# W_down on two bank sets, emptied into four output blocks, and tail tiles with roots of their own

## The chip, the cores and the metric

One core of a Trainium2 chip runs the kernel. The metric is the device time of one execution in microseconds (us). One execution was also recorded by the hardware profiler; the times in the rows below count from the start of its span.

## What is computed

One decoder layer on x of 1024 positions by 1024 channels, in fp32: two token mixers side by side, their projection W_out, and an MLP, each with a norm before and after it. The change touches the last line of it alone:

```
h = rms_norm(x, norm_ffn_pre[i])
f = jnp.square(jax.nn.relu(jnp.einsum("bld,df->blf", h, w_up[i])))
x = x + rms_norm(jnp.einsum("blf,fd->bld", f, w_down[i]), norm_ffn_post[i])
```

W_down is 4096 x 1024, f is 1024 x 4096. rms_norm divides each row by the root of its mean square and multiplies by a weight.

## The kernel before, in words

Every dense product is done with split operands: each fp32 operand is a high part (rounded) and a low part (the rest), and mm3 (L123) issues three matmuls, high x high, high x low, low x high.

The W_down product (L1097 to L1316) goes over 4096 inner columns in eight groups of 512. Seven of them use Winograd's form of Strassen's scheme: the product of 2 x 2 blocks with seven block products instead of eight. The outputs are four blocks of 512 x 512 (two row halves, two column halves). With P1 to P7 the block products, the four blocks are P1 + P2, P1 + P6 + P5 + P3, P1 + P6 + P7 - P4 and P1 + P6 + P7 + P5. The combinations of f were spilled to memory (fsp) by the stage before; those of W_down (t1 to t4) are formed here, as differences of blocks on VectorE (w_block, L1128). The groups are gathered in sets SG (L1101): one group, then two, two, two; the eighth group is multiplied plainly in the tail.

In the loop at L1210 each step is one block product of one group: 4 row tiles x 2 inner blocks x 3 matmuls = 24 matmuls of 512 columns. Two steps ahead of it, d_prep (L1163) makes the operands ready: f_load (L1144) brings a piece of f into one of two staging buffers (L1217 issues it three steps ahead), ScalarE rounds it to the high part, GpSimd forms the low part (f_piece, L1148, three pairs of buffers fh and fl); ScalarE and VectorE do the same for the block of W_down. A product has a bank set of 128 x 2048 in PSUM, two sets in turn (tag pd, L1222). ORD (L1103) is the order of the products, and MORE (L1104) names those that continue on the bank set of another: P2 is added to P1 in the bank, P3 to P5. After the last group of a set, flush (L1184) empties the bank set into one of seven accumulators accs (L1097), by a copy on ScalarE in the first set and by an addition on VectorE later; in the last set, five additions among the accumulators, the final sums, form the four blocks.

The tail (L1296 on) takes 8 row tiles of 128 x 1024, each in two halves. For each half: 12 matmuls of the eighth group (pl, L1304, eight banks, in the place of the two bank sets), VectorE adds them to the block, ScalarE sums the squares, GpSimd multiplies by the norm's weight. When a tile has both halves, VectorE computes the reciprocal root by an integer seed and three Newton steps (chain, L1247, rstd_steps, L136), and finishes each half: multiply by the root, add x, and an output transfer (finish, L1260). TAIL (L1245) takes the first six tiles in pairs: operations of the chain then have two columns a partition and two tensor inputs; the last two have chains of their own, whose Newton steps use the form with one tensor input. The chain and the finishes of a tile are queued (todo) and issued between later halves, up to a number of steps given to some (L1268); VectorE's order in the tail is the order of the code (L1296). In the stage ahead, the scheduler sets the order on each engine.

Of the kernel before, what the change touches and what calls it, by code (L numbers as in the profile page):

```python
# [8 lines left out]
F32 = mybir.dt.float32  # L9
# [6 lines left out]
P = 128  # L16
SEQ = 1024
D = 1024
# [15 lines left out]
N_STAGE = 2  # L34
# [6 lines left out]
N_CARRY = 2  # L41
# [15 lines left out]
def hymba_kernel(ctx, tc, x, norm_mix_pre, w_in, gm_ln_w, gm_ln_b, gm_w_s, gm_b_s,  # L57
# [24 lines left out]
    pe, act, dve, pool = [Engine(e) for e in (nc.tensor, nc.scalar, nc.vector, nc.gpsimd)]  # L82

    def pool_of(stack, name, **k):
        return stack.enter_context(tc.tile_pool(name=name, bufs=1, reuse_waits="tile", **k))
# [7 lines left out]
    stage = pool_of(uctx, "stage")  # L93
# [36 lines left out]
    def rstd_base(ss, n):  # L130
        nsmall[0] += 1
        b = const.tile([P, 1], F32, tag="rb", bufs=4, name=f"rb{nsmall[0]}")
        dve.tensor_scalar(b, ss, 0.5 / n, 0.5 * EPS, op0=ALU.mult, op1=ALU.add)
        return b

    def rstd_steps(ss, n, base=None):  # L136
        nsmall[0] += 1
        i = nsmall[0]
        w = ss.shape[-1]
        v = const.tile([P, w], F32, tag=f"rv{w}", bufs=2 if w == 1 else 1, name=f"rv{i}")  # L140
        r = const.tile([P, w], F32, tag=f"rr{w}", bufs=4 if w == 1 else 1, name=f"rr{i}")
        t = const.tile([P, w], F32, tag=f"rt{w}", bufs=2 if w == 1 else 1, name=f"rt{i}")
        ti = const.tile([P, w], I32, tag=f"rti{w}", bufs=2 if w == 1 else 1, name=f"rti{i}")
        yield r
        if base is None:
            dve.tensor_scalar(v, ss, 0.5 / n, 0.5 * EPS, op0=ALU.mult, op1=ALU.add)
        else:
            dve.tensor_scalar(v, ss, 0.5 / n, base, op0=ALU.mult, op1=ALU.add)
        yield
        dve.tensor_scalar(ti, v.bitcast(I32), 1, None, op0=ALU.logical_shift_right)  # L150
        yield
        dve.tensor_scalar(r.bitcast(I32), ti, -1.0, RSQRT_SEED, op0=ALU.mult, op1=ALU.add)
        for _ in range(3):
            yield
            if w == 1:
                dve.tensor_scalar(t, r, r, v, op0=ALU.mult, op1=ALU.mult)
            else:
                dve.tensor_mul(t, v, r)
                dve.tensor_mul(t, t, r)
            yield  # L160
            if w == 1:
                dve.tensor_scalar(r, t, 1.5, r, op0=ALU.subtract, op1=ALU.mult)
            else:
                dve.scalar_tensor_tensor(r, t, 1.5, r, op0=ALU.subtract, op1=ALU.mult)
# [87 lines left out]
    for what in PRO_LOADS:  # L252
# [4 lines left out]
        else:  # L257
            t = int(what)
# [611 lines left out]
    def tt(eng, out_, a, b, op):  # L870
        eng.tensor_tensor(out_, a, b, op=op)

    def sub(eng, out_, a, b):
        tt(eng, out_, a, b, ALU.subtract)

    def add(eng, out_, a, b):
        tt(eng, out_, a, b, ALU.add)
# [213 lines left out]
    dpool = pool_of(ctx, "dpool")  # L1091
    apool = pool_of(ctx, "apool")
# [1 line left out]
    now["nwp"] = pool_of(ctx, "nw2")  # L1094
    pctx2 = stack()
    psum2 = pool_of(pctx2, "psum2", space=bass.MemoryType.PSUM)
    accs = {i: apool.tile([P, 4, 512], F32, name=f"acc{i}") for i in range(1, 8)}  # L1097
    last = N_GROUP - 1


    SG = [(0,), (1, 2), (3, 4), (5, 6), (last,)]  # L1101
    sg_of = {g: (n, gs.index(g)) for n, gs in enumerate(SG) for g in gs}
    ORD = (1, 5, 2, 3, 6, 7, 4)  # L1103
    MORE = {2: 1, 3: 5}  # L1104
    raws, wts, pcs = {}, {}, {}
    wr_loads = []

# [20 lines left out]
    def w_block(g, key):  # L1128
        if key[0] == "b":
            return rows(g, int(key[1]) - 1)[:, :, int(key[2]) - 1, :]  # L1130
        if (g, key) not in wts:
            one, two = {"t1": ("b12", "b11"), "t2": ("b22", "t1"), "t3": ("b22", "b12"),
                        "t4": ("t2", "b21")}[key]
            a_, b_ = w_block(g, one), w_block(g, two)
            t_ = a_ if key == "t4" else dpool.tile([P, 2, 512], F32, tag="wt", bufs=4, name=f"w{key}_{g}")
            sub(dve, t_, a_, b_)
            wts[g, key] = t_
        return wts[g, key]
# [3 lines left out]
    frs = {}  # L1142

    def f_load(name, src):  # L1144
        frs[name] = stage.tile([P, 2, 512], F32, tag="ws", bufs=N_STAGE, name="fr" + name)
        nc.sync.dma_start(frs[name], src)

    def f_piece(name, tags=("fh", "fl"), bufs=3):  # L1148
        fr = frs[name]
        hl = piece([P, 2, 512], "f" + name) if tags is None else \  # L1150
            tuple(dpool.tile([P, 2, 512], F32R, tag=t_, bufs=bufs, name=f"f{i}" + name)
                  for i, t_ in enumerate(tags))
        split(*hl, fr)
        return hl
# [13 lines left out]

    seq = [(n, g, i) for n, gs in enumerate(SG[:-1]) for i in ORD for g in gs]
    us, ffs = [], []  # L1170
# [10 lines left out]
    floads = [lambda g=g, i=i: d_load(g, i) for n, g, i in seq]  # L1181
    floads += [lambda i=i: last_load(i) for i in range(4)]

    def flush(n, i, ps):  # L1184
        a_ = accs
        if n == 0:
            act.copy(a_[i], ps)
            return
        if n == len(SG) - 2 and i == 4:
            sub(dve, a_[4], a_[4], ps)  # L1190
            return
        add(dve, a_[i], ps, a_[i])
        if n < len(SG) - 2:
            return
        if i == 6:
            add(dve, a_[6], a_[6], a_[1])
            add(dve, a_[3], a_[3], a_[6])
        elif i == 7:
            add(dve, a_[7], a_[7], a_[6])
            sub(dve, a_[4], a_[7], a_[4])  # L1200
            add(dve, a_[5], a_[5], a_[7])

    w_load(0, 0)
    floads[0]()
# [5 lines left out]
    for m, (n, g, i) in enumerate(seq):  # L1210
        gs = SG[n]
        k = m - seq.index((n, gs[0], ORD[0]))
        if k == len(gs):
            w_load(n + 1, 0)
        elif k == 5 * len(gs) + 1:
            w_load(n + 1, 1)
        floads[m + 3]()  # L1217
        preps[m + 2]()
        (fh, fl), (h, l) = pcs[g, i]
        if g == gs[0]:  # L1220
            banks[i] = banks[MORE[i]] if i in MORE else \
                psum2.tile([P, 4, 512], F32, tag="pd", bufs=2, name=f"pd{n}_{i}")  # L1222
        ps = banks[i]
        for t in range(4):
            tsl = slice(t * P, (t + 1) * P)
            for q in range(2):
                mm3(ps[:, t, :], fh[:, q, tsl], fl[:, q, tsl], h[:, q, :], l[:, q, :],
                    g == gs[0] and q == 0 and i not in MORE, g == gs[-1] and q == 1,
                    skip_group_check=i in MORE)
        if g == gs[-1]:  # L1230
            flush(n, i, ps)
    for m in range(len(seq) + 2, len(preps)):
        if m + 1 < len(preps):
            floads[m + 1]()
# [4 lines left out]
    psum3 = pool_of(ctx, "psum3", space=bass.MemoryType.PSUM)  # L1239

    def acc(t, dh):
        return accs[((2, 3), (4, 5))[t // 4][dh]][:, t % 4, :]

    xqs, sss, chains, rs = [], {}, {}, {}
    TAIL = ((0, 1), (2, 3), (4, 5), (6,), (7,))  # L1245

    def chain(ts):  # L1247

        nsmall[0] += 1
        w = len(ts)  # L1250
        v = const.tile([P, w], F32, tag=f"tv{w}", bufs=2, name=f"tv{nsmall[0]}")
        dve.tensor_tensor(v, sss[ts][:, :, 0], sss[ts][:, :, 1], op=ALU.add)
        yield
        steps = rstd_steps(v, D)
        r = next(steps)
        for j, t in enumerate(ts):
            rs[t] = r[:, j:j + 1]
        yield from steps
# [9 lines left out]
    def some(k):  # L1268
        while k and todo:
            if todo[0]() == "done":  # L1270
                todo.pop(0)
            k -= 1
# [23 lines left out]
    dve.held = True  # L1296
    for ts in TAIL:
        ss = sss[ts] = const.tile([P, len(ts), 2], F32, tag=f"st{len(ts)}", bufs=4, name=f"ssy{ts[0]}")
        for j, t in enumerate(ts):
            tsl = slice(t * P, (t + 1) * P)  # L1300
            for dh in range(2):
                ds_ = slice(dh * 512, (dh + 1) * 512)
                a_ = acc(t, dh)
                ps = psum3.tile([P, 512], F32, tag="pl", bufs=8, name=f"pl{t}{dh}")  # L1304
                for i in range(4):
                    mm3(ps, ffs[i][0][:, tsl], ffs[i][1][:, tsl], us[i][0][:, dh, :],
                        us[i][1][:, dh, :], i == 0, i == 3)
                add(dve, a_, ps, a_)
                junk = now["tok"].tile([P, 512], BF16, tag="junk", bufs=1, name=f"yj{t}{dh}")
                act.activation(junk, a_, AF.Square, accum_out=ss[:, j, dh:dh + 1])  # L1310
                pool.tensor_tensor(a_, a_, wfpost[:, ds_], op=ALU.mult)
                some(6 if len(ts) > 1 else 12)
        todo.append(chain_op(ts))
        for t in ts:
            todo += [finish_op(t, 0), finish_op(t, 1)]
# [29 lines left out]
```

## Time and profile before

| what | us |
|---|---|
| median of three runs | 1087.95 |
| lowest and highest | 1083.33, 1088.11 |
| the profiled execution | 1084.19 |
| its span, first to last instruction | 1082.5 |

In the span TensorE is busy for 1026.2 us (95%), VectorE for 761.1 (70%), ScalarE for 500.1 (46%) and GpSimd for 389.0 (36%). The W_down stage begins near 748.5 us, the tail near 1017.6. In the rows PE is TensorE, PEld its weight loads, DVE VectorE, ACT ScalarE, POOL GpSimd, and SPq the queue of transfers issued by SyncE. A tile's name on the left of the arrow is what is written: pd and pl are banks, acc the accumulators, wld the low part of a W_down block, f the parts of an f piece, fr its staging, wt a difference of W_down blocks, rv, rti, rr, rt the small operands of a root.

### The profile page before, as it was taken

To read this page: it belongs to the slowest core of one execution; us is meant where nothing else is said; L and a number is where in the kernel's file an instruction comes from. 1 tells how busy PE (TensorE), PEld (TensorE's weight loads), DVE (VectorE), ACT (ScalarE), POOL (GpSimd) and SP (SyncE) were. 2 spreads that over 40 slices of the span, in tenths; PEclk is the share of its full clock that TensorE was granted. 3 is DMA by queue.
4 is the path that set the end of the run, shared out by engine and by line. 5 is a ranking of instruction groups with operands and counts; after the bars stand their busy time and mean duration, and the time that the engine had idled before them with its cause. 6 is when DMAs were issued, how large, how long until landed. Compare 5 with 4: busy or idle time off the path is not lost.

```text
span 1082.5 us, 13146 instructions
## 1 busy us (share of the span) xinstructions
PE 1026.2 (95%) x4735; PEld 835.8 (77%) x4735; DVE 761.1 (70%) x1246; ACT 500.1 (46%) x673; POOL 389.0 (36%) x197
## 2 busy tenths in 40 slices
PE   5999997999899989999999999999999999999795
PEld 4877676777678878888788888887888888888684
DVE  5746887267986745668477777776758778767957
ACT  5546453353463533676444444445753333333221
POOL 5543525233545151500011111113444444444543
PEclk9999998999999999999999999999999999999898
DMA  6443412324852133766767777767654354434413
GB/s 199 135 120 134 153 43 78 107 68 139 260 169 76 40 117 98 227 220 193 244 195 230 226 225 229 227 220 254 249 191 172 96 173 134 143 108 172 152 39 116
DMA packets 139560, 172.40 MB, mean 159 GB/s; under 512 B 8308, under 2 KB 83176, under 8 KB 139496
## 3 DMA queue, kind: packets, MB, share of 16 engines
q1 hardware_dynamic: 105064, 152.70, 42.7%
q10 hardware_dynamic: 34432, 18.88, 6.0%
q8 instruction: 37, 0.61, 0.2%
q14 instruction: 27, 0.22, 0.1%
HBM read 129.05 MB, written 42.50 MB: 158 GB/s over the span
## 4 chain that ended last, share of the span: by engine, by line
PE 71%; DVE 16%; DMA 4%; ACT 4%; issue 3%; SPq 1%; POOL 1%; DVEq 0%; ACTq 0%
PE pd L73 22%; PE pe L73 8%; PE puC L73 8%; PE puB L73 8%; PE pso L73 8%; PE puD L73 4%; PE pl L73 3%; DVE v L73 3%; PE psv L73 2%; PE psz L73 2%; DMA gg<-acd 2%; DVE acc L73 2%; DVE gg L73 1%; PE psB L73 1%; DVE rt L73 1%
## 5 line engine op out<-in xcount | busy, mean ns | idle before, releaser
L73 POOL TENSOR_TENSOR wl<-ws,wh 128x1024 fp32r<-128x1024 f32 x64 | 160.6, 2516 | 209.3 <-ACT wh L73 198.1
L73 PE MATMUL pd<-whd,f 128*128 128x512 f32 x752 | 231.5, 389 | 0.0
L73 POOL TENSOR_TENSOR f<-fr,f 128x1024 fp32r<-128x1024 f32 x47 | 117.7, 2507 | 143.2 <-ACT f L73 134.9
L73 PEld LDWEIGHTS pd<-whd,f 128*128 128x128 f32 x752 | 141.2, 188 | 29.1
L73 PE MATMUL pd<-wld,f 128*128 128x512 f32 x376 | 146.3, 389 | 0.0
L73 POOL TENSOR_TENSOR wlb<-sa,whb 128x1024 fp32r<-128x1024 f32 x16 | 38.5, 2406 | 223.7 <-ACT whb L73 189.1
L73 ACT CAST f<-fr 128x1024 fp32r<-128x1024 f32 x47 | 49.4, 1054 | 137.8 <-PE pd L73 134.0
L73 ACT CAST wh<-ws 128x1024 fp32r<-128x1024 f32 x72 | 75.2, 1046 | 73.2 <-PE pso L73 14.4
L73 PEld LDWEIGHTS pd<-wld,f 128*128 128x128 f32 x376 | 70.6, 188 | 14.8
L73 DVE TENSOR_TENSOR wld<-wt,whd 128x1024 fp32r<-128x1024 f32 x28 | 60.8, 2173 | 27.0 <-ACT whd L73 22.9
L73 ACT ACTIVATE u<-u 128x512 f32<-128x512 f32 (+1 forms) x66 | 44.3, 672 | 54.1 <-DVE u L73 48.5
L73 DVE TENSOR_TENSOR wld<-wr,whd 128x1024 fp32r<-128x1024 f32 x21 | 46.3, 2205 | 28.4 <-ACT whd L73 28.4
L73 DVE TENSOR_TENSOR acc<-pd,acc 128x2048 f32<-128x2048 f32 x20 | 45.7, 2287 | 10.1 <-PE pd L73 10.1
L73 ACT ACT_TABLE_LOAD x30 | 38.5, 1283 | 30.8 <-DVE carry L73 8.1
L73 PE MATMUL pe<-hTh,wh 128*128 128x512 f32 x128 | 50.3, 393 | 0.0
L73 PE MATMUL pe<-hTh,wl 128*128 128x512 f32 x128 | 49.9, 390 | 0.0
L73 PE MATMUL pe<-hTl,wh 128*128 128x512 f32 x128 | 49.9, 389 | 0.0
L73 DVE TENSOR_TENSOR u<-puB,s 128x512 f32<-128x512 f32 x32 | 22.1, 691 | 31.9 <-PE puB L73 16.7
L73 DVE TENSOR_SCALAR gg<-gg,acs 128x128 f32<-128x128 f32 x64 | 21.2, 389 | 22.3 <-DMA gg<-acd 22.3
L73 DVE TENSOR_TENSOR wlc<-sa,whc 128x1024 fp32r<-128x1024 f32 x16 | 29.4, 1835 | 6.1 <-ACT whc L73 6.1
L73 PE MATMUL pso<-wh,mixbh 128*128 128x512 f32 x64 | 28.0, 438 | 4.2 <-DVE hTl L73 2.9
L73 ACT ACTIVATE f<-f 128x512 f32<-128x512 f32 x32 | 20.2, 633 | 25.0 <-DVE f L73 24.5
(345 smaller groups left out, 2706.5 us busy)
## 6 DMA issues: line engine op xcount, KB each, us to landing
fr<-fsp SPq DMA_DIRECT2D x49, 512.0 KB, 3.8
ws<-in_w_in_dram SPq DMA_DIRECT2D x40, 512.0 KB, 4.1
wu<-in_w_up_dram ACTq DMA_DIRECT2D x32, 512.0 KB, 4.2
wr<-in_w_down_dram SPq DMA_DIRECT2D x32, 512.0 KB, 5.9
fsp<-c SPq DMA_DIRECT2D x42, 256.0 KB, 2.0
ws<-in_w_out_dram SPq DMA_DIRECT2D x16, 512.0 KB, 3.3
ws<-in_w_up_dram SPq DMA_DIRECT2D x16, 512.0 KB, 4.2
fsp<-u SPq DMA_DIRECT2D x28, 256.0 KB, 3.3
```

The costliest lines, as they stand in the source:

```text
L73: ins = fn(*a, **k)
```

## The change

The order of the products becomes 1, 5, 6, 3, 7, 2, 4. P6, P7 and P4 continue on the bank set of P1, so that it holds P1, then P1 + P6, then P1 + P6 + P7, then that and P4 (t4 is formed with the opposite sign); P3 continues on that of P5; P2 has a fresh set. INTO says to which of four output blocks the content of the bank set is added after each product. The first content for a block is copied by ScalarE, the other 24 of 28 are added by VectorE. The final sums are gone, and with them three accumulators. In the room of these, f pieces beyond the first two are staged in four buffers of their own (fr) instead of the two shared ones, and fh and fl have four places instead of three. In the tail each of the eight tiles has its own root: a base operation takes the first half's sum of squares as soon as it is there, and the chain begins with the second half's. The numbers given to some become 15, and 10 at the first half of the last tile, which moves one finish of the seventh tile behind the last addition.

```diff
-    accs = {i: apool.tile([P, 4, 512], F32, name=f"acc{i}") for i in range(1, 8)}
+    accs = {k: apool.tile([P, 4, 512], F32, name=f"acc{k}") for k in (11, 12, 21, 22)}
...
-    ORD = (1, 5, 2, 3, 6, 7, 4)
-    MORE = {2: 1, 3: 5}
+    ORD = (1, 5, 6, 3, 7, 2, 4)
+    MORE = {6: 1, 3: 5, 7: 1, 4: 1}
+    INTO = {1: 11, 5: 22, 6: 12, 3: 12, 7: 22, 2: 11, 4: 21}
...
-                        "t4": ("t2", "b21")}[key]
+                        "t4": ("b21", "t2")}[key]
...
-            t_ = a_ if key == "t4" else dpool.tile([P, 2, 512], F32, tag="wt", bufs=4, name=f"w{key}_{g}")
+            t_ = b_ if key == "t4" else dpool.tile([P, 2, 512], F32, tag="wt", bufs=4, name=f"w{key}_{g}")
...
-        frs[name] = stage.tile([P, 2, 512], F32, tag="ws", bufs=N_STAGE, name="fr" + name)
+        pool_, tag, bufs = (stage, "ws", N_STAGE) if len(frs) < N_CARRY else (dpool, "fr", 4)
+        frs[name] = pool_.tile([P, 2, 512], F32, tag=tag, bufs=bufs, name="fr" + name)
...
-    def f_piece(name, tags=("fh", "fl"), bufs=3):
+    def f_piece(name, tags=("fh", "fl"), bufs=4):
...
-    def flush(n, i, ps):
-        a_ = accs
-        if n == 0:
-            act.copy(a_[i], ps)
-            return
-        if n == len(SG) - 2 and i == 4:
-            sub(dve, a_[4], a_[4], ps)
-            return
-        add(dve, a_[i], ps, a_[i])
-        if n < len(SG) - 2:
-            return
-        if i == 6:
-            add(dve, a_[6], a_[6], a_[1])
-            add(dve, a_[3], a_[3], a_[6])
-        elif i == 7:
-            add(dve, a_[7], a_[7], a_[6])
-            sub(dve, a_[4], a_[7], a_[4])
-            add(dve, a_[5], a_[5], a_[7])
+    done = set()
+
+    def flush(i, ps):
+        a_ = accs[INTO[i]]
+        if INTO[i] in done:
+            add(dve, a_, ps, a_)
+        else:
+            act.copy(a_, ps)
+            done.add(INTO[i])
...
-                psum2.tile([P, 4, 512], F32, tag="pd", bufs=2, name=f"pd{n}_{i}")
+                psum2.tile([P, 4, 512], F32, tag=f"pd{(n + (i != 1)) % 2}", bufs=1, name=f"pd{n}_{i}")
...
-    TAIL = ((0, 1), (2, 3), (4, 5), (6,), (7,))
+    TAIL = tuple((t,) for t in range(8))
+    tbase = {}
...
+        if w == 1:
+            steps = rstd_steps(sss[ts][:, 0, 1:2], D, tbase[ts])
+            rs[ts[0]] = next(steps)
+            yield from steps
+            return
...
-                some(6 if len(ts) > 1 else 12)
+                some(7 if len(ts) > 1 else 10 if t == 7 and dh == 0 else 15)
+                if len(ts) == 1 and dh == 0:
+                    tbase[ts] = rstd_base(ss[:, 0, 0:1], D)
```

## Rows read from the trace of the kernel before

**Rows 1.** Table by stretches: busy us of each engine (instructions), granted clock, DMA share, GB/s.
```profile
790.00:865.00 75.00, 75.00 (x332) 62.15 (x331) 54.95 (x29) 28.95 (x29) 33.99 (x14) 1.00 0.45 153
865.00:940.00 75.00, 75.00 (x332) 62.12 (x331) 56.75 (x29) 28.05 (x28) 33.63 (x14) 1.00 0.43 140
940.00:1017.60 77.60, 77.60 (x344) 64.25 (x344) 60.38 (x28) 28.06 (x29) 34.28 (x14) 1.00 0.45 158
1017.60:1025.90 8.30, 1.96 (x10) 1.30 (x8) 8.24 (x4) 2.10 (x2) 5.49 (x2) 0.79 0.44 176
1025.90:1069.50 43.60, 43.58 (x184) 35.62 (x184) 28.51 (x66) 10.14 (x28) 18.67 (x15) 0.96 0.16 61
1069.50:1082.50 13.00, 0.00 (x0) 0.00 (x0) 8.33 (x26) 1.45 (x4) 3.41 (x3) 0.66 0.32 120
```

**Rows 2.** Waits of TensorE, from 756 and from 1017 us: total, times, longest.
```profile
PE pd L73 <- DVE wld L73: 1.7, 1, 1.7
...
PE pl L73 <- DVE acc L73: 6.3, 1, 6.3
```

**Rows 3.** Timeline of TensorE, 1017 to 1069: start, us, operation, [idle before, releaser].
```profile
1017.58 0.39 PE L73 MATMUL pl<-whdl,f0l 128*128 128x512 f32 x1
...
1019.17 0.39 PE L73 MATMUL pl<-wldl,f0l 128*128 128x512 f32 x1
1025.89 0.80 PE L73 MATMUL pl<-whdl,f0l 128*128 128x512 f32 x1 [6.34 <-DVE acc L73]
...
1069.09 0.39 PE L73 MATMUL pl<-whdl,f1l 128*128 128x512 f32 x1
```

**Rows 4.** Timeline of VectorE between 1000 and 1026 us.
```profile
1000.38 6.69 DVE L73 TENSOR_TENSOR acc<-acc,acc 128x2048 f32<-128x2048 f32 x2
...
1011.48 8.88 DVE L73 TENSOR_TENSOR acc<-acc,acc 128x2048 f32<-128x2048 f32 x3
1020.29 3.36 DVE L73 TENSOR_TENSOR wldl<-wr,whdl 128x1024 fp32r<-128x1024 f32 x1
1023.57 2.27 DVE L73 TENSOR_TENSOR acc<-acc,pd 128x2048 f32<-128x2048 f32 x1
```

**Rows 5.** Operations on the accumulators: count, ns min/median/max, first and last start.
```profile
L73 DVE TENSOR_TENSOR acc<-pd,acc x20: 2277/2288/2292, 800.2 to 1008.1; 128x2048 f32<-128x2048 f32 x20
...
L73 ACT COPY acc<-pd x7: 1857/1863/1872, 757.0 to 790.1; 128x2048 f32<-128x2048 f32 x7
```

**Rows 6.** Last f piece, in the timelines of SyncE, ScalarE, GpSimd; then ScalarE's wait.
```profile
1016.03 0.36 SPq L1146 DMA_DIRECT2D frl<-fpl  x1
...
1023.12 1.04 ACT L73 CAST f0l<-frl 128x1024 fp32r<-128x1024 f32 x1 [4.47 <-DMA frl<-fpl]
...
1024.24 2.35 POOL L73 TENSOR_TENSOR f1l<-frl,f0l 128x1024 fp32r<-128x1024 f32 x1 [1.69 <-ACT f0l L73]
...
ACT f L73 <- PE pd L73: 134.0, 41, 3.4
```

**Rows 7.** Timelines of TensorE and VectorE at the start of the stage.
```profile
756.55 0.50 PE L73 MATMUL pd<-wld,whf 128*128 128x512 f32 x1 [1.69 <-DVE wld L73]
...
756.42 3.41 DVE L73 TENSOR_TENSOR wld<-wr,whd 128x1024 fp32r<-128x1024 f32 x1
...
762.03 3.43 DVE L73 TENSOR_TENSOR wt<-wr 128x1024 f32<-128x1024 f32 x1
```

**Rows 8.** Timelines of VectorE, then GpSimd, in the tail.
```profile
1062.99 1.26 DVE L73 TENSOR_TENSOR rt<-rv,rr 128x2 f32<-128x2 f32 x1
...
1071.00 0.27 DVE L73 TENSOR_SCALAR rt<-rr,rv 128x1 f32<-128x1 f32 x1
...
1074.07 0.68 DVE L73 TENSOR_TENSOR acc<-pl,acc 128x512 f32<-128x512 f32 x1
1075.60 0.16 DVE L73 TENSOR_TENSOR tv<-ssy 128x1 f32<-128x1 f32 x1 [0.85 <-ACT yj L73]
...
1078.11 1.41 DVE L73 SCALAR_TENSOR_TENSOR acc<-acc,rr,wr 128x512 f32<-128x512 f32 x2
...
1062.95 1.28 POOL L73 TENSOR_TENSOR acc<-acc,wfpost 128x512 f32<-128x512 f32 x1 [0.63 <-ACT yj L73]
...
1070.75 1.26 POOL L73 TENSOR_TENSOR acc<-acc,wfpost 128x512 f32<-128x512 f32 x1 [0.36 <-ACT yj L73]
```

More of the change, by code (lines that the diff above doesn't have):

```diff
@@ L1230, in hymba_kernel @@
         if g == gs[-1]:
-            flush(n, i, ps)
+            flush(i, ps)
     for m in range(len(seq) + 2, len(preps)):
@@ L1241, in acc @@
     def acc(t, dh):
-        return accs[((2, 3), (4, 5))[t // 4][dh]][:, t % 4, :]
+        return accs[((11, 12), (21, 22))[t // 4][dh]][:, t % 4, :]
     xqs, sss, chains, rs = [], {}, {}, {}
-    TAIL = ((0, 1), (2, 3), (4, 5), (6,), (7,))
+    TAIL = tuple((t,) for t in range(8))
+    tbase = {}
     def chain(ts):
```

## The prediction

> **What bounds the kernel now.** I read the table by stretches first [rows 1]. From 790 to 1017.6 us the W_down products run, and TensorE is busy for the whole of it at a granted clock of 1.00 while VectorE is busy for 73 to 78%: TensorE is the bound, and removing VectorE work there buys nothing by itself. Then come 8.30 us in which TensorE is busy for 1.96, 43.60 us in which it is full again but at a mean clock of 0.96, and 13.00 us after its last matmul, with VectorE work and output transfers alone. Second, TensorE's own waits: between 756 and 1017 us one wait of 1.7 us, and from 1017 on one of 6.3 us, "until VectorE acc" [rows 2]. TensorE's timeline gives its place: the tail products (pl) start at 1017.58, directly behind the last product P4; after eight of them it stands, and resumes at 1025.89 [rows 3]. Third, VectorE's timeline around the hole shows what it was doing: two final sums at 1000.38 (6.69 us), three at 1011.48 (8.88 us), a late weight split at 1020.29 (3.36 us), and only then, at 1023.57, the emptying of P4's bank, which ends at 1025.84 [rows 4]. TensorE starts 0.05 us behind that. So the reader should see a queue: P4 had been in its bank since 1017.6, but its reader stood behind 15.6 us of sums.
>
> **The final sums go.** Five SBUF-to-SBUF sums and 21 bank-emptying operations on VectorE become 24 emptyings; on ScalarE seven copies become four [rows 5]. That is two operations fewer on VectorE in all, about 4.6 us of busy time, and 3 x 1.86 = 5.6 us on ScalarE; both count as nothing inside the full stretch. What counts is the order at the end. P2 is emptied while P4 runs, the last weight splits no longer stand behind sums, and P4 can be emptied in the 2.3 us behind its end, by about 1020. TensorE has twelve matmuls of the first tail product to run in that time, if their operands are there.
>
> **Are they there?** Before, the last f piece came late too: its load was issued at 1016.03, ScalarE could copy it at 1023.12, GpSimd finished its low part at 1026.6 [rows 6]. The reason is staging in two buffers, each freed by GpSimd's split, and three fh/fl pairs: ScalarE waited 41 times for TensorE to free one (134.0 us) [rows 6]. With four of each the pieces run one product (24 matmuls, 5.45 us at the pitch below) further ahead, and a load two staging places further still: the load is issued about 3 x 5.45 = 16 us earlier, and the low part is done before 1017.6. I therefore take the hole as closed to zero. Bounds: zero, and 4 us if a VectorE operation of up to 3.4 us [rows 4, 7] is in front of P4's emptying.
>
> **What closing it gives.** The pitch of matmuls at full clock is (1019.17 - 1017.58)/7 = 0.227 us [rows 3]. 192 tail matmuls take 43.6 us; started at 1017.58 they end at 1061.3. Before, the last one started at 1069.09 and ended at 1069.48. TensorE's end moves by 8.2 us: 6.5 of standstill, and 1.7 of lower clock behind it, for the granted clock was 0.79 in the hole and 0.96 in the stretch behind it [rows 1], against 1.00 in the stretch ahead; the first matmul behind the hole shows 0.80 us instead of 0.39 [rows 3].
>
> **The tail: own roots.** Before, the last bank addition began at 1074.07 [rows 8], 4.6 us behind TensorE's end: VectorE was late. Now each tile costs VectorE two bank additions (0.68 each), a base operation (0.2, as the one at 1075.60), nine small operations (nine of this form lie between 1075.80 and 1078.11, 2.3 us) and two finishes (1.41) [rows 8], together 5.3 us; TensorE delivers a tile every 24 x 0.227 = 5.45 us. But a root can only begin when ScalarE's sum of squares for the tile's second half is there: VectorE waited 0.85 us for that at 1075.60 [rows 8]. GpSimd's two multiplications of 1.28 us [rows 8], back to back from some 0.8 us behind that addition, end at 3.4 us, the root at 0.85 + 2.3 = 3.15, so the finish waits 0.25 more. The round from one second-half addition to the next is 0.85 + 2.3 + 0.25 + 1.41 + 0.2 + 0.68 = 5.7 us against 5.45: VectorE falls behind by about 0.25 us a tile. On top, the second half's addition stands behind the first half's, the previous tile's root and its finishes (0.68 + 2.3 + 1.41 + 0.2 = 4.6 us where TensorE needs 2.72), 1.9 us late from the start. Stepping the eight tiles from 1017.6 on in this way, with one finish of the seventh tile moved behind it, the last addition begins at 1064.1, 2.8 us behind TensorE's end instead of 4.6: a gain of 1.8. From there to the span's end took 1082.5 - 1074.07 = 8.43 us; without the operation that added the halves it takes 8.25. Moving the second finish of the seventh tile behind the last addition (0.7 us) is hidden by ScalarE's 0.85 us there.
>
> **GpSimd's neighbourhood.** A root operation with two tensor inputs (pairs) took 1.26 us at 1062.99 and ended with GpSimd's operation of 1062.95; the form with one tensor input (single tiles) took 0.27 us at 1071.00, inside GpSimd's operation that began at 1070.75 [rows 8]. So I charge no blocking to the new roots; that they are blocked all the same is rival C. The Trainium skill (SBUF — State Buffer, Who interferes with whom) speaks against the change here: besides operations with two SBUF inputs it lists tensor_scalar, the form of the new roots, among those that can enter the mode that shares ports with GpSimd and then fully block. By that alone each root would stand behind one GpSimd operation, and the sum would be that of rival C; the row at 1071.00 does not agree, for operands of one element a partition.
>
> **Start of the stage.** The order becomes 1, 5, 6, 3, 7, 2, 4, so the third product needs t2 instead of b21. In the first group three emptyings (P3, P7, P2) move from ScalarE (1.86 us) to VectorE (2.29 us), where a product takes only 5.45 us and the same bank is wanted again one product later; VectorE operations of 3.41 and 3.43 us stand in that neighbourhood [rows 7]. Worst: 3.4 + 2.3 = 5.7 us against 5.45, three times 0.3. The three buffers' worth of sums saved is given to staging, so the tiles of this stage lie elsewhere, over tiles of the stage before whose last spills land late; a load that waits for them could hold a piece by up to 5 us. On the other side, the wait of 1.7 us for P5's weights [rows 2], which ended at 756.55 [rows 7], could go, since the early loads no longer share two buffers. I take zero, between -2 and +5. The bank order alternates strictly as before, also between groups, so no new wait for a bank arises in the groups of two, where a product lasts 10.9 us.
>
> **The sum.** 1082.5 - 8.2 - 1.8 - 0.2 = 1072.3 us of span, 10.2 less, or 1084.19 - 10.2 = 1074.0 for the execution of the profile. The timed runs lie from 1083.33 to 1088.11 with the median near the upper end, 3.8 above the profiled one; I set the forecast a little above the sum, at 1075.0, since a median of the new kernel may fall in either place. Own range 1070 to 1079.
>
> **The rivals.** (A) The hole stays in part: P4's emptying queued behind a blocked split, 4 us standstill and 1.2 of lower clock: 1080. For it: VectorE's order is still left to the scheduler. Against: the 15.6 us of sums that made the queue are gone. Chance 0.10. (B) A stall in the first group by moved buffers or late emptying, 2 to 5 us: 1077 to 1080. Chance 0.10. (C) Every new root is held up for one GpSimd operation, as the paired root at 1062.99 was [rows 8]: 1.3 us a tile, the round 7.0 us, 1.3 x 7 = 9 us: 1084, no change. The row at 1071.00 speaks against. Chance 0.05. (This is what the list in the Trainium skill, SBUF — State Buffer, Who interferes with whom, would make of it.) (D) Slower: pieces further ahead put VectorE's splits beside GpSimd's everywhere, and VectorE becomes the bound of the long stretch. It is busy 60.38 of 77.60 us [rows 1], that is 4.24 us a product of 5.45; were each of its splits and block differences stretched to the 3.43 us of the longest [rows 7], a product of one group would cost one split, four sevenths of a difference and half an emptying, 3.4 + 2.0 + 1.1 = 6.5. It decides from 5.45 us; at 5.9, over 45 products, it costs 20 us and the kernel is at 1094. Against: the step from 4.24 is large, and the amount of VectorE work falls. Chance 0.05. (E) Both open gains come: the wait of 1.7 us at the start goes, and the last addition follows TensorE's end at once (2.8 us less), as it would if a finish and the root were spread better than I step them: 1074.0 - 4.5 = 1069.5. Chance 0.08. The forecast keeps 0.62.
>
> **How the numbers follow.** The range takes in A, B and E, and on each side about 1.5 us of the timed runs' spread: 1068 to 1082. A measurement can tell about 0.5% from no change, 5.4 us. Faster by more holds the forecast, E, and most of A and B: 0.83. Same: the rest of these and C, 0.11. Slower: D and a rest, 0.06.
>
> **What would show it.** Right: no TensorE wait over 1 us behind 1017 us; P4's emptying begun within 0.5 us of its end; granted clock 1.00 through the tail; last matmul near 1061; last addition about 3 us behind it; root operations near 0.2 us beside GpSimd. Wrong: a TensorE wait for VectorE, ScalarE or a load between 755 and 800 us; a VectorE share near 100% in the long stretch; roots that end with GpSimd's operations.

## The result, and the profile after

The changed kernel took 1078.92 us in the median of six runs (1076.11 to 1082.01), the kernel before 1087.65 in six; the ratio is 0.9929, interval 0.9902 to 0.9957 (it isn't the quotient of the two medians, which would be 0.992). The changed kernel was measured against the kernel before twice more, both times on one chip (below, e5_after and e12_after_again): 0.9958 [0.9942, 0.9974] and 0.9955 [0.9934, 0.9976]. So the change is worth 0.4 to 0.7%, 4 to 9 us, where I had worked out 10.2. The profiled execution took 1076.11 us, its span is 1074.4.

First the waits of TensorE from 740 us on (total, times, longest), as in [rows 2]:

```profile
PE pd L73 <- DVE acc L73: 7.9, 1, 7.9
PE pd L73 <- DVE wld L73: 0.8, 1, 0.8
```

The wait of 6.3 us in the tail is gone, that of 1.7 us is 0.8, and there is a new one of 7.9 us, on the banks of the long stage (pd). The table by stretches, with the columns of [rows 1], shows where:

```profile
772.60:780.57 7.97, 0.05 (x2) 0.01 (x1) 7.97 (x4) 2.09 (x2) 7.92 (x3) 0.76 0.65 231
780.57:790.00 9.43, 9.43 (x35) 7.72 (x36) 7.87 (x6) 2.00 (x2) 1.29 (x1) 0.84 0.19 57
790.00:865.00 75.00, 75.00 (x332) 62.12 (x332) 54.56 (x29) 29.08 (x29) 32.48 (x15) 1.00 0.45 154
...
940.00:1017.60 77.60, 77.60 (x344) 64.29 (x343) 52.66 (x25) 30.44 (x31) 37.40 (x16) 1.00 0.40 136
1021.50:1065.20 43.70, 43.66 (x193) 35.84 (x191) 34.22 (x98) 10.87 (x30) 18.79 (x15) 1.00 0.21 82
1065.20:1074.40 9.20, 0.00 (x0) 0.00 (x0) 5.62 (x16) 0.72 (x2) 1.58 (x2) 0.78 0.30 115
```

From the bottom up: the stretch without TensorE at the end is 9.2 us (13.0 before), the tail is full at clock 1.00 in 43.7 us (51.9 before with its hole, from 1017.6 to 1069.5), the long stretch is as before. The loss lies in the first group: from 772.60 to 780.57 TensorE stands, while VectorE and GpSimd are busy for all of it, and behind that the granted clock is 0.84. TensorE's timeline, columns of [rows 3]:

```profile
780.57 0.79 PE L73 MATMUL pd<-whd,f 128*128 128x512 f32 x1 [7.92 <-DVE acc L73]
...
1021.48 0.39 PE L73 MATMUL pl<-whdl,f0l 128*128 128x512 f32 x1
...
1064.77 0.39 PE L73 MATMUL pl<-whdl,f1l 128*128 128x512 f32 x1
```

The matmul at 780.57 is the first of P2, the sixth product, which wants the banks of P5 and P3. P3 had ended near 767.0. VectorE, then GpSimd, between 763 and 781 us:

```profile
763.80 1.21 DVE L73 TENSOR_TENSOR wld<-wr,whd 128x1024 fp32r<-128x1024 f32 x1
764.93 3.42 DVE L73 TENSOR_TENSOR wld<-wt,whd 128x1024 fp32r<-128x1024 f32 x1
768.28 3.43 DVE L73 TENSOR_TENSOR wt<-wr,wt 128x1024 f32<-128x1024 f32 x1
771.64 3.39 DVE L73 TENSOR_TENSOR wld<-wr,whd 128x1024 fp32r<-128x1024 f32 x1
774.95 3.36 DVE L73 TENSOR_TENSOR wt<-wr,wt 128x1024 f32<-128x1024 f32 x1
778.23 2.28 DVE L73 TENSOR_TENSOR acc<-pd,acc 128x2048 f32<-128x2048 f32 x1
...
763.78 16.74 POOL L73 TENSOR_TENSOR f<-fr,f 128x1024 fp32r<-128x1024 f32 x5 [4.39 <-ACT f L73]
```

P3's emptying (778.23) stands behind four weight operations, three of which belong to the next set. Each takes 3.4 us instead of 1.21: GpSimd runs five splits back to back, 16.74 / 5 = 3.35 us each, and the four VectorE operations end 3.3 to 3.4 us apart (768.35, 771.71, 775.03, 778.31), one to each split. Four times 3.4 is 13.6 us; behind the unhindered one of 763.80 the next begins 1.13 us later, so by my estimate four would take 4.5 and the emptying would be over by 764.93 + 4.5 + 2.3 = 771.7, ahead of P7's end at 772.6. By this estimate the whole wait comes from that stretch of 9 us.

At the other end, VectorE empties P4 at 1021.68, while TensorE is already in the tail, and the last f piece's low part (GpSimd) is done at 1019.6, ahead of the tail's start:

```profile
1021.68 2.29 DVE L73 TENSOR_TENSOR acc<-pd,acc 128x2048 f32<-128x2048 f32 x1 [1.01 <-PE pd L73]
...
1017.19 2.40 POOL L73 TENSOR_TENSOR f1l<-frl,f0l 128x1024 fp32r<-128x1024 f32 x1 [2.75 <-ACT f0l L73]
```

and the tail's tiles, VectorE and one GpSimd row, answer to [rows 8]:

```profile
1035.28 0.69 DVE L73 TENSOR_TENSOR acc<-pl,acc 128x512 f32<-128x512 f32 x1 [0.41 <-PE pl L73]
1035.89 0.21 DVE L73 TENSOR_SCALAR rv<-ssy,rb 128x1 f32<-128x1 f32 x1
...
1036.51 0.27 DVE L73 TENSOR_SCALAR rt<-rr,rv 128x1 f32<-128x1 f32 x1
...
1039.64 0.69 DVE L73 TENSOR_TENSOR acc<-pl,acc 128x512 f32<-128x512 f32 x1
1040.72 0.69 DVE L73 TENSOR_TENSOR acc<-pl,acc 128x512 f32<-128x512 f32 x1 [0.39 <-PE pl L73]
...
1066.18 0.68 DVE L73 TENSOR_TENSOR acc<-pl,acc 128x512 f32<-128x512 f32 x1
...
1035.77 2.54 POOL L73 TENSOR_TENSOR acc<-acc,wfpost 128x512 f32<-128x512 f32 x2 [3.05 <-ACT yj L73]
```

The last addition (1066.18) is 1.0 us behind TensorE's end (1064.77 + 0.39).

### The profile page after: what moved, and what is told of

Its sections match the earlier page's. It is cut to its first block, busy times and chain, and to the rows that moved or that the text cites. A ratio compares the mean times of both kernels' runs of the same rounds, so it can differ in the third digit from the quotient of the medians.

```text
span 1074.4 us, 13172 instructions
## 1 busy us (share of the span) xinstructions
PE 1019.9 (95%) x4735; PEld 832.6 (77%) x4735; DVE 760.8 (71%) x1265; ACT 494.6 (46%) x670; POOL 387.1 (36%) x197
## 5 line engine op out<-in xcount | busy, mean ns | idle before, releaser
L73 DVE TENSOR_TENSOR wld<-wt,whd 128x1024 fp32r<-128x1024 f32 x28 | 63.5, 2267 | 27.2 <-ACT whd L73 27.2
L73 DVE TENSOR_TENSOR acc<-pd,acc 128x2048 f32<-128x2048 f32 x24 | 54.9, 2287 | 13.6 <-PE pd L73 13.6
L73 ACT CAST whd<-wt 128x1024 fp32r<-128x1024 f32 x28 | 29.3, 1046 | 5.7 <-DVE wt L73 2.8
```

The lines of the kernel that those rows point to most:

```text
L73: ins = fn(*a, **k)
```

## The experiments

For each kernel I read four marks in its trace: the first matmul of the long stage (pd), the first and last of the tail (pl), the last addition of a pl bank, and the span's end. The differences say which part of the stage moved; the last column but one is their sum. Ahead of the first mark TensorE's instructions come in the same order in all fourteen traces, yet the mark fell anywhere from 743.9 to 750.3 us.

| kernel | first pd | to first pl | to last pl | to last addition | to end | stage | ratio to before |
|---|---|---|---|---|---|---|---|
| before | 748.75 | 268.8 | 51.5 | 5.0 | 8.4 | 333.7 | 1 |
| after | 743.94 | 277.5 | 43.3 | 1.4 | 8.2 | 330.5 | 0.9929 |
| e1_hold | 747.44 | 270.6 | 43.3 | 1.4 | 8.2 | 323.6 | 0.9880 |
| e2_fewbuf | 744.67 | 270.4 | 44.2 | 3.3 | 8.2 | 326.1 | 0.9881 |
| e3_nosums | 747.29 | 268.9 | 44.2 | 5.6 | 8.4 | 327.0 | 0.9931 |
| e4_pairs | 749.75 | 278.5 | 43.3 | 5.0 | 8.4 | 335.2 | 0.9994 |
| e5_after | 746.91 | 278.3 | 43.3 | 1.4 | 8.2 | 331.2 | 0.9958 |
| e6_before | 750.25 | 268.8 | 51.5 | 5.2 | 8.4 | 333.9 | 1 |
| e7_late_act | 749.12 | 280.6 | 43.3 | 1.4 | 8.2 | 333.5 | 0.9960 |
| e8_roots | 746.28 | 270.5 | 52.8 | 2.4 | 8.2 | 333.9 | 0.9959 |
| e9_few_hold | 746.30 | 275.2 | 45.4 | 1.5 | 8.2 | 330.2 | 0.9943 |
| e10_late | 744.36 | 272.6 | 43.3 | 1.4 | 8.2 | 325.5 | 0.9866 |
| e11_late_again | 745.91 | 272.1 | 43.3 | 1.4 | 8.2 | 325.1 | 0.9886 |
| e12_after_again | 745.07 | 279.0 | 43.3 | 1.4 | 8.2 | 331.9 | 0.9955 |

My theory after the result: the new wait needs two things, P3's emptying behind weight operations for later products in VectorE's order, and GpSimd splitting several pieces in a row beside them. Rivals: the order alone; the three emptyings moved from ScalarE to VectorE; the moved buffers.

**e1_hold: VectorE's order taken from the code in the first eight steps of the loop.**

```diff
     banks = {}
+    dve.held = True
     for m, (n, g, i) in enumerate(seq):
+        if m == 8:
+            dve.held = False
```

> The changed kernel, with VectorE kept to the order of the code through the first eight products, so that the emptying of P3's bank stands ahead of the next set's weight work. Queue theory (P2 stood 7.9 us because P3's emptying was queued behind four weight operations of 3.4 us): the wait goes, and with it about 1.5 us of lower clock; stage about 9 us shorter than in the changed kernel, time near 1069.5 against 1078.9, ratio to the kernel before near 0.984. Load theory (the first group has too much VectorE work whatever its order): a wait of 5 us or more shows at P2 or at a later product, ratio near 0.992 as in the changed kernel.

Measured: 1072.97 us (1072.06 to 1075.18), ratio 0.9880 [0.9863, 0.9897]. Waits of TensorE, VectorE at P3's emptying, and GpSimd:

```profile
PE pd L73 <- DVE acc L73: 2.5, 1, 2.5
...
770.60 2.29 DVE L73 TENSOR_TENSOR acc<-pd,acc 128x2048 f32<-128x2048 f32 x1 [3.11 <-ACT f L73]
...
767.02 10.81 POOL L73 TENSOR_TENSOR f<-fr,f 128x1024 fp32r<-128x1024 f32 x4 [5.29 <-ACT f L73]
```

GpSimd still runs four splits in a row, but the emptying now stands ahead of the later weight operations, starts as P3 ends (near 770.5), and keeps its 2.29 us inside that run (one of its inputs is a bank). The 7.9 us are gone; a wait of 2.5 us at 811 us, in the second set, is what is left beside 0.8 us for weights, and the stage is 6.9 us shorter than in the changed kernel instead of the expected 9. The order is held only up to the eighth step, and that wait is of the same kind: the emptying of P1, which had ended near 798, begins at 808.83, behind weight operations of up to 3.4 us. So the emptyings that moved to VectorE cost TensorE nothing in the first group when they are in time; and since this edit changes no buffer, the moved buffers don't make the wait.

**e2_fewbuf: staging as before the change, everything else changed.**

```diff
-        pool_, tag, bufs = (stage, "ws", N_STAGE) if len(frs) < N_CARRY else (dpool, "fr", 4)
-        frs[name] = pool_.tile([P, 2, 512], F32, tag=tag, bufs=bufs, name="fr" + name)
+        frs[name] = stage.tile([P, 2, 512], F32, tag="ws", bufs=N_STAGE, name="fr" + name)
...
-    def f_piece(name, tags=("fh", "fl"), bufs=4):
+    def f_piece(name, tags=("fh", "fl"), bufs=3):
```

> The changed kernel with the staging of the kernel before: two shared f buffers and three fh/fl places. Burst theory (four buffers let ScalarE and GpSimd run five f splits back to back, and GpSimd's splits stretch the VectorE operations ahead of P3's emptying from 1.2 to 3.4 us): the first group's wait falls from 7.9 us to under 3. If the order of VectorE alone is to blame: 5 us or more stay. At the end, if the four buffers were needed there: the last f piece is late again, low part done near 9 us behind P4's end, and TensorE stands 3 to 5 us in the tail; if the removed sums alone closed the hole: under 1 us.

Measured: 1072.90 us (1070.59 to 1077.01), ratio 0.9881 [0.9862, 0.9900]. VectorE, then GpSimd:

```profile
765.10 1.21 DVE L73 TENSOR_TENSOR wt<-wr,wt 128x1024 f32<-128x1024 f32 x1
766.24 1.21 DVE L73 TENSOR_TENSOR wld<-wt,whd 128x1024 fp32r<-128x1024 f32 x1
767.49 1.23 DVE L73 TENSOR_TENSOR wt<-wr,wt 128x1024 f32<-128x1024 f32 x1
768.63 1.22 DVE L73 TENSOR_TENSOR wld<-wr,whd 128x1024 fp32r<-128x1024 f32 x1
770.50 2.29 DVE L73 TENSOR_TENSOR acc<-pd,acc 128x2048 f32<-128x2048 f32 x1 [0.66 <-PE pd L73]
...
768.91 5.56 POOL L73 TENSOR_TENSOR f<-fr,f 128x1024 fp32r<-128x1024 f32 x2 [7.08 <-ACT f L73]
```

The same four weight operations, in another order, stand ahead of the emptying, but GpSimd has nothing to split beside them, each takes 1.2 us, and the emptying now waits for P3 to end. So the order alone doesn't make the wait. The hole at the tail stays closed too, to 0.6 us, although the last piece's low part is late again: the deeper staging was not needed for that. TensorE again waits 1.7 us for P5's weights, as in [rows 2], and the last addition is 1.9 us later behind the last tail matmul than with deep staging.

**e3_nosums: the kernel before without its five final sums.**

```diff
         add(dve, a_[i], ps, a_[i])
-        if n < len(SG) - 2:
-            return
-        if i == 6:
...
-            add(dve, a_[5], a_[5], a_[7])
```

> The kernel before without its five final sums, which are left out, so the four blocks are not complete; all else as before. Queue theory: P4's emptying begins within 1 us of P4's end, TensorE's wait in the tail falls from 6.3 us to under 1, TensorE's last matmul comes about 8 us earlier, ratio near 0.992. Late-piece theory (the last f pieces hold the hole as much as the sums): a wait of 3 to 6 us for GpSimd or ScalarE stays, ratio 0.995 to 1.

Measured: 1078.76 us (1076.00 to 1082.16), ratio 0.9931 [0.9912, 0.9951]. TensorE's wait and P4's emptying:

```profile
PE pl L73 <- DVE acc L73: 0.6, 1, 0.6
...
1016.36 2.29 DVE L73 TENSOR_TENSOR acc<-acc,pd 128x2048 f32<-128x2048 f32 x1 [1.01 <-PE pd L73]
```

With the sums gone and nothing else changed, the hole of 6.3 us is 0.6, and the tail from its first to its last matmul is 44.2 us instead of 51.5. So the sums made nearly all of the hole, and their price is 7.2 us in the medians (1085.99 - 1078.76), 6.7 in the stage's own time.

**e4_pairs: the changed kernel with the old paired tail.**

```diff
-    TAIL = tuple((t,) for t in range(8))
+    TAIL = ((0, 1), (2, 3), (4, 5), (6,), (7,))
```

> The changed kernel with the old tail: three pairs of tiles and two single ones, and the old numbers of queued steps. Root theory (own roots let VectorE keep pace): the last addition begins 3 to 5 us behind TensorE's last matmul instead of 1.0, and the time is 3 to 4 us above the changed kernel's, near 1082.5. Rival (the lateness of VectorE before came from the hole, not from the pairs): within 1 us of the changed kernel.

Measured: 1086.20 us (1082.66 to 1087.26), ratio 0.9994 [0.9983, 1.0005]. The first group (278.5 us) gives back what the tail wins (43.3), and the end is as late as before: without the roots the change is worth nothing. I had expected 3 to 4 us above the changed kernel; the stage is 4.7 us longer, 3.7 of them behind the last tail matmul and 1.0 in the first group, which this edit doesn't touch. The rows, VectorE's and then GpSimd's, show a paired root held up until GpSimd's operation ends, as at 1062.99 in [rows 8], and then the last addition, 4.6 us behind TensorE's end:

```profile
1065.47 1.27 DVE L73 TENSOR_TENSOR rt<-rv,rr 128x2 f32<-128x2 f32 x1
...
1076.55 0.68 DVE L73 TENSOR_TENSOR acc<-pl,acc 128x512 f32<-128x512 f32 x1
...
1065.43 1.29 POOL L73 TENSOR_TENSOR acc<-acc,wfpost 128x512 f32<-128x512 f32 x1 [0.63 <-ACT yj L73]
```

That hold is 1.1 us; the rest of what the pairs cost (their finishes come in a bunch, and the finish moved behind the last addition goes back ahead of it) I did not take apart.

**e5_after and e6_before: the two kernels once more, on another chip than e1 to e4.**

> The changed kernel once more, for a second profile on the same chip as the others. Its stage from the first W_down matmul to the end was 330.5 us against 333.8 before, 3.3 us less, but the median was 8.7 us lower. If the 4.8 us that its profile had won before that stage were one execution's clock: stage 330 to 331 again, start of the stage between 747 and 750 us, ratio 0.993 to 0.997. If they come with the program each time: start near 744 again and ratio 0.990 to 0.993.

> The kernel before once more, one profile: the stage from the first W_down matmul to the end 333 to 335 us, TensorE's wait in the tail 6.3 us, by either theory. If the start of the stage depends on the single execution it may lie anywhere from 744 to 750 us; if it comes with the program, within 1 us of 748.7.

Measured: 1081.40 us (1076.60 to 1083.25) and 1085.90 (a single run; the median of that chip's runs of before is 1085.44), ratio 0.9958. The waits of 7.9 and 0.8 us, and of 6.4 and 1.7 us, came again, and the stage's time differs by 2.7 us, close to the first pair's 3.3. The rest of the 8.1 us between the first pair's spans lies ahead of the stage, which the change doesn't touch.

**e7_late_act: the first 21 f pieces in the two shared buffers, and ScalarE's order taken from the code up to step 4.**

```diff
-        pool_, tag, bufs = (stage, "ws", N_STAGE) if len(frs) < N_CARRY else (dpool, "fr", 4)
+        pool_, tag, bufs = (stage, "ws", N_STAGE) if len(frs) < 21 else (dpool, "fr", 4)
...
+    act.held = True
     w_load(0, 0)
...
+        if m == 4:
+            act.held = False
```

> The changed kernel with the two shared staging buffers for the first 21 f pieces and the four own ones only after them, and with ScalarE kept to the order of the code for the first four products, so that P5's weights are rounded ahead of later f pieces. Burst theory: no wait over 1 us in the first two sets, as in the run with few buffers, and no late piece at the end, as in the changed kernel; stage near 322 us, ratio near 0.985. If instead more memory for staging is harmful or useless at any time: no better than the run with few buffers, 0.988.

Measured: 1082.12 us (1077.97 to 1084.36), ratio 0.9960 [0.9945, 0.9976]: no better. ScalarE's timeline shows why:

```profile
772.61 1.05 ACT L73 CAST f<-fr 128x1024 fp32r<-128x1024 f32 x1 [10.47 <-DMA fr<-fsp]
...
774.51 1.86 ACT L73 COPY acc<-pd 128x2048 f32<-128x2048 f32 x1
```

In the code's order a copy of a bank stands behind a cast of an f piece that waited 10.47 us for its load; TensorE waited 3.1 us for that copy, and 3.3 us for an emptying later. Two things were changed at once here; e10 separates them.

**e8_roots: the kernel before with roots of its own for each tile.**

```diff
-    TAIL = ((0, 1), (2, 3), (4, 5), (6,), (7,))
+    TAIL = tuple((t,) for t in range(8))
...
+        if w == 1:
+            steps = rstd_steps(sss[ts][:, 0, 1:2], D, tbase[ts])
...
```

> The kernel before with own roots for all tiles, and nothing else of the change. Root theory (pairs make VectorE late by 3 to 4 us at the end whatever lies ahead): the last addition begins under 2 us behind TensorE's last matmul instead of 4.6, ratio 0.996 to 0.997. Rival (own roots only pay where the hole of 6.3 us is closed, since VectorE is late through it): ratio 0.999 to 1.

Measured: 1081.26 us (1078.47 to 1084.26), ratio 0.9959 [0.9942, 0.9976]. The hole of 6.3 us stays, the last addition comes 2.4 us behind the last matmul's start instead of 5.0 (2.0 behind its end, just missing my "under 2"). The interval leaves out the rival's 0.999 to 1. But in this trace the 2.6 us are lost again (1.3 in the tail, 1.6 in the groups), while the medians show 4.2: how much the roots are worth alone this run doesn't settle. With the hole closed, e4 and after have the same tail in front of them, and there the roots, with the one finish moved behind the last addition, give 4.97 + 8.39 - 1.41 - 8.21 = 3.74 us.

**e9_few_hold: the edits of e1 and e2 together.**

> The changed kernel with both remedies: f staging as before the change (two shared buffers for all pieces, three places of fh and fl) and VectorE's order in the first eight steps of the W_down loop taken from the code. If each remedy alone has already removed the whole 7.9 us wait and the rest is the same, both together give what each gave alone, 0.988 of the kernel before (about 1072 to 1073 us), with no TensorE wait over 1 us between 740 and 800 us but for the 1.7 us at P5. If the wait of 2.5 us that the ordered variant had between 800 and 830 us comes from the deep staging, it is absent here and the ratio is 0.985 to 0.987. If ordering VectorE costs something of its own beside shallow staging (a weight piece behind an emptying), a wait of 1 to 4 us appears and the ratio is 0.989 to 0.992.

Measured: 1080.07 us (1076.26 to 1084.71), ratio 0.9943 [0.9924, 0.9961]: each remedy alone is worth 13 us against before, both together 6. TensorE waits 2.6 us for ScalarE, and 0.8 us in the tail for the last f piece's low part. TensorE's wait in the tail, then TensorE, VectorE, ScalarE:

```profile
PE pl L73 <- POOL f1l L73: 0.8, 1, 0.8
...
767.12 0.50 PE L73 MATMUL pd<-whd,f 128*128 128x512 f32 x1 [2.58 <-ACT acc L73]
...
759.85 3.43 DVE L73 TENSOR_TENSOR wt<-wr,wr 128x1024 f32<-128x1024 f32 x1
...
763.31 1.05 ACT L73 CAST whd<-wt 128x1024 fp32r<-128x1024 f32 x1 [3.87 <-DVE wt L73]
...
765.21 1.86 ACT L73 COPY acc<-pd 128x2048 f32<-128x2048 f32 x1
```

P5 had ended near 759; its copy stands on ScalarE behind two casts, the first of which waits for a difference that VectorE in the code's order forms late (759.85) and that is stretched beside a GpSimd split. The third expectation had the size of the wait; that the ratio would be 0.994, through it and through waits of 2.1 us at 814 us and 1.4 us in the tail, it had not. The wait at 814 us falls on the same product as e1's at 811 us, with shallow staging here, so it doesn't come from the deep staging.

**e10_late: the change of buffers of e7 without the hold.** One number is changed (21 in place of N_CARRY, the first line of e7's edit).

> The changed kernel, but the first 21 f pieces (the first group and the start of the second set) are staged in the two shared buffers as before the change, and only later ones in four of their own; four places of fh and fl stay, and no order is held. If the 7.9 us wait comes from the four staging buffers in the first group, it is gone: 0.988 of the kernel before (1072 to 1073 us), GpSimd's splits between 755 and 780 us in pairs at most, P3's emptying within 2 us of its end. If the four places of fh and fl alone suffice for ScalarE and GpSimd to run ahead, the wait stays at 4 to 8 us and the ratio is 0.992 to 0.996. If the scheduler's order for VectorE falls out differently, the wait may move to another product; the ratio then goes by what the trace shows, 0.99 to 0.996, as in the run that held ScalarE's order too.

Measured: 1072.12 us (1070.64 to 1075.17), ratio 0.9866 [0.9842, 0.9891]. TensorE's waits, then VectorE and GpSimd:

```profile
PE pd L73 <- DVE wld L73: 1.7, 1, 1.7
PE pd L73 <- POOL f L73: 1.1, 1, 1.1
PE pd L73 <- DVE acc L73: 0.4, 1, 0.4
...
763.01 1.23 DVE L73 TENSOR_TENSOR wld<-wt,whd 128x1024 fp32r<-128x1024 f32 x1 [0.75 <-issue]
765.95 2.02 DVE L73 TENSOR_TENSOR wt<-wr,wt 128x1024 f32<-128x1024 f32 x1 [1.71 <-DMA wr<-in_w_down_dram]
767.88 1.21 DVE L73 TENSOR_TENSOR wld<-wr,whd 128x1024 fp32r<-128x1024 f32 x1
769.02 1.21 DVE L73 TENSOR_TENSOR wt<-wr,wt 128x1024 f32<-128x1024 f32 x1
770.20 2.29 DVE L73 TENSOR_TENSOR acc<-pd,acc 128x2048 f32<-128x2048 f32 x1
...
764.48 2.40 POOL L73 TENSOR_TENSOR f<-fr,f 128x1024 fp32r<-128x1024 f32 x1 [10.12 <-ACT f L73]
```

This separates the causes best. VectorE's program has the very order of the changed kernel here: the four weight operations, then P3's emptying. Only the pieces come one or two at a time instead of five: beside the four operations GpSimd has a single split (764.48), one of the four is longer (2.02 us), and the emptying starts at 770.20, right at P3's end. The four places of fh and fl, and the other product order, are in this kernel too, so neither makes the wait by itself.

**e11_late_again and e12_after_again: e10 and the changed kernel side by side on one chip.**

> The kernel with the four staging buffers taken up only from the 22nd f piece on, a second time, beside the changed kernel on the same chip. If its gain is real and not a matter of one chip, it is again at 0.985 to 0.989 of the kernel before (about 1072 us) and 5 to 8 us under the changed kernel of the same call, as the 7.9 us wait less its own waits of 1.1 and 0.4 us would have it. If the difference came from the chip, the two are within 3 us of each other.

> The changed kernel, a third time, for the comparison on one chip: 0.993 to 0.996 of the kernel before (1078 to 1082 us), with the wait of 7.9 us at the fifth product's end. If the earlier results were a matter of the chip, it falls to 0.988 to 0.990, or the wait is absent.

Measured: 1072.46 us (1071.05 to 1077.79), ratio 0.9886 [0.9860, 0.9913], against 1080.57 us (1077.40 to 1086.64), 0.9955. Of the 8.1 us between them 6.9 are in the stage (331.9 and 325.1): 5.9 are waits of TensorE (8.7 against 2.8), and the rest lies in the lower clock behind the waits: in the changed kernel P2, behind the long wait, took 8.4 us instead of 5.4 (granted clock 0.64), while in the other P5 lost 2.0 us behind its wait of 1.7 (0.76). So three variants of one small edit (e1, e2, e10) beat both kernels, at 1072 to 1073 us; they can't be told from each other.

## Why the prediction was right, and where not

The time came out in the range (1068 to 1082) and in the forecast's own range, 3.9 us above the forecast. But in part that was luck: it came there by two errors of opposite sign, and rival B, which I gave 0.10, came true beside the forecast, with 7.9 us of standstill instead of its 2 to 5. One of my own signs of being wrong, a TensorE wait for VectorE between 755 and 800 us, was there.

**The hole (8.2 us): right in size, half right in cause.** From the first tail matmul to the last it is 43.3 us instead of 51.5, 8.2 us less; granted clock 1.00, no wait. That the queue of sums made most of it is shown by e3 (7.3 of the 8.2). The pieces did come earlier, the last low part 1.9 us ahead of the tail's first matmul. But that they must, the second half of my argument, falls: in e2 and e3 that part is done 8.3 and 7.9 us behind the tail's first matmul (9.0 before), and the wait is 0.6 us, near the zero end of my bounds of zero to 4; earlier pieces are worth 0.9 us here (44.2 against 43.3). I had reckoned with the twelve matmuls of the first tail product, the last of which need that piece. With late pieces the scheduler's order is another: in e9 the first matmul that waits for the last low part is the 29th of the tail, and it waits 0.8 us.

**The tail (1.8 + 0.2 us predicted): 3.6 + 0.2 measured.** The last addition is 1.0 us behind TensorE's end, not 2.8. The mis-sized term is the 0.85 us that I put into VectorE's round for ScalarE's sum of squares; it made the round 5.7 us, and 0.25 us a tile over seven tiles are the 1.8 us in between. In the rows the root of a tile (1035.89) stands behind the next tile's first addition (1035.28), which covers that time; the round is paced by TensorE at 1040.72 - 1035.28 = 5.44 us with 0.4 us to spare, and nothing adds up over the tiles. The roots' operations take 0.15 to 0.28 us inside GpSimd's 2.54 us (1035.77), so rival C is out. At one element a partition this trace doesn't show the blocking that the Trainium skill (SBUF — State Buffer, Who interferes with whom) holds possible for tensor_scalar, which it makes depend on the operands. The rule of the Trainium skill, in the same section, that an operation with two SBUF inputs contends with a GpSimd instruction that reads SBUF agrees with the weight operations at 764.93 and behind it (3.4 us instead of 1.21), and with e4's paired root (1.27 us).

**The start of the stage (zero predicted, -2 to +5): 8.7 us lost.** This is the step that failed. The first five products and what follows up to the tail took 277.5 us instead of 268.8: 7.9 us of new wait, less 0.9 of the old one at P5's or now P6's weights (which the staging did shorten, as I had held possible), and 1.7 of lower clock and small remainders; behind the hole the granted clock was 0.84 over 9.4 us, the first matmul took 0.79 us, and P2 took 7.0 us instead of 5.4. My bound for late emptying was one blocked operation ahead of it, 3.4 + 2.3 us against 5.45, "three times 0.3". Two things were missing. The queue: I counted one operation ahead of an emptying, and the scheduler had put four there. And what fills GpSimd: I had counted the four staging buffers as a gain at the tail, and had their cost only as loads that might land late (up to 5 us; no run shows such a price for the moved buffers). In fact they let ScalarE and GpSimd take five pieces in a row at the start, and that run stretched all four. Both factors are needed: with the order mended (e1) or the run broken up (e2, e10) the wait is gone.

**Rival D had the mechanism at the wrong place.** It set VectorE's operations at 3.43 us each all over the long stretch. There VectorE is busy for 54.56 of 75 us, as before (54.95): TensorE's pace spaces the pieces out, one split in 5.44 us, and the VectorE operations beside them took 2.1 to 2.6 us, in the kernel before too. In the changed kernel several operations of 3.4 us in a row came only where the buffers are filled for the first time.

**The sum.** Predicted -10.2. By the marks: +8.7 - 8.2 - 3.6 - 0.2 = -3.3 us for the stage in the profiled pair (-2.7 in the second). The spans differ by 8.1, because the first mark lay 4.8 us earlier, ahead of all that was changed; the timed medians of the three measurements differ by 8.7, 4.0 and 5.8. The rest of my expected gain is thus not missing but given back in the first group, and e10 has it: 325.5 against 333.7, 8.2 us in the stage, 2.0 less than worked out. One side figure was wrong without entering the sum: five sums fewer and three emptyings more free 15.6 - 3 x 2.29 = 8.7 us of VectorE's time by [rows 4, 5], not 4.6.

## What to carry to other kernels

More staging buffers need not only move a late transfer earlier. Here, at the first filling, they turned ScalarE and GpSimd loose in one run, and the VectorE operations with both inputs in SBUF were stretched for as long as the run lasted. So when a bank's reader is moved to an engine that is held up in this way, write down the whole queue ahead of it in program order, price each entry at its stretched time, and compare with the time until the bank is wanted. And give deeper buffers only where the pieces are late (here the end), not where they are already early; at the end they moved the last addition forward by 0.9 + 1.9 us in the traces (e2 against e10), but the times of e2 and e10 can't be told apart. Two remedies that each work by changing an order need not add up (e9).

## What the runs showed of the hardware

- A VectorE operation of 128 x 1024 with both inputs in SBUF took 1.21 us alone and 3.36 to 3.43 us in a run of GpSimd splits, one such operation to each split (splits 3.35 us each instead of 2.4). An emptying with one input in PSUM kept its 2.29 us in such a run.
- Ahead of the stage, with TensorE's instructions in the same order, the first matmul of the stage came between 743.9 and 750.3 us in fourteen traces. The granted clock differed too; the stretch from 150 to 200 us, columns of [rows 1], in before and then in after (0.90 and 0.97):

```profile
150.00:200.00 50.00, 43.21 (x205) 35.54 (x204) 35.24 (x65) 17.91 (x26) 17.12 (x8) 0.90 0.21 58
```

```profile
150.00:200.00 50.00, 42.49 (x211) 35.40 (x210) 34.34 (x64) 17.85 (x26) 17.17 (x8) 0.97 0.22 63
```

So two single profiles of kernels that differ only later can differ by 6 us ahead of the difference; a stage is compared from its own first mark. What sets the clock in those stretches stays open.
